# Second feed-forward layer: half of the second parts of groups 9 and 10 as a third, half as wide chunk of seven products, the other half plain at the end

## Chip, cores and metric

One NeuronCore of one Trainium2 chip runs the whole program in one launch. The metric is the device time of one execution, in microseconds (us); the figure for a kernel is the median of several runs. One execution of the kernel before was recorded by the hardware profiler, and all rows below come from it.

## What is computed

A decoder layer of width 1024 over 1024 tokens in 32-bit floating point: a SwiGLU feed-forward half-step, a mixing layer, a second SwiGLU half-step and a final RMSNorm. What the change touches is the second half-step and the norm behind it:

```
def swiglu(h, w_gate, w_up, w_down):
    return (jax.nn.silu(h @ w_gate) * (h @ w_up)) @ w_down
...
        h = modulate(rms_norm(x, ffn2_norm[l]), sh3, sc3)
        x = x + 0.5 * g3[:, None, :] * swiglu(h, ffn2_w_gate[l], ffn2_w_up[l], ffn2_w_down[l])
    return rms_norm(x, final_norm)
```

`w_gate` and `w_up` are 1024x2816, `w_down` is 2816x1024. The kernel cuts the inner width 2816 into 11 groups of 256, numbered 0 to 10. The **first part** of a group is its gate and up products, `silu(h @ w_gate) * (h @ w_up)`; the **second part** is its share of the product with `w_down`.

## The kernel before, in words

**Numbers.** Every 32-bit operand is kept as two `float32r` halves, a rounded one and the rest. A product is three matmuls, high by high, high by low and low by high (`mm3`). Tokens are cut into two halves of 512 (`h` = 0 and 1), and a matmul is 128 by 128 weights against 128x512 activations, into one PSUM bank.

**Seven products.** Groups 1 to 10 of the first part run by Winograd's form of Strassen's scheme. The activations are cut into four blocks A11, A12, A21, A22 (token half by half of the inner dimension). From them come four combinations S1 to S4, sums and differences of blocks, each made from earlier ones, and seven products take the place of eight: A11, S1, S2, S4, S3, A12, A22, in that order (`SEVEN`), in three PSUM accumulators named B, C and A (`fbd_0C` is accumulator C for output column pair 0). The weights need combinations too. They are made in DRAM-to-SBUF transfers: a raw tile is loaded by a DMA that SyncE (SP) issues, and another block is added onto it by an accumulating DMA that GpSimd (POOL) issues (line 173). `Weights.seven` makes seven weight tiles of four blocks: the raw tile x takes one addition, the raw tile y takes three, each after the tile before it was split. `Weights.pump` splits a raw tile into a weight tile `w` with a `CAST` on ScalarE (ACT) and a subtraction on VectorE (DVE), in the fixed order of the granules, whenever one of the weight slots comes free. Three raw tiles are held at a time.

**Second part.** `seven` leaves a group's A blocks, and its S combinations, in DRAM (`Kept`): each block is split into its two halves on ACT and DVE into a tile of the pool `movA` (20 tiles of 512 KB) and written by SP (`kept9A` is a write of an A block of group 9, `kept9S` of an S combination). `down7` then does the second part of four groups at once, a *chunk*: chunk 0 is groups 1 to 4, chunk 1 groups 5 to 8. `fetch_chunk` reads the kept blocks back, one block of one group per DMA of 512 KB (`fb1lA` is a block A of group 1), into tiles that the first part, or the chunk before, has just finished with. A chunk has two passes p = 0 and 1; each does the seven products of four of the eight output columns `d`, 7 products x 2 columns x 4 groups x 3 = 168 matmuls. Each finished result goes through one more addition on DVE and is added into `x` by a `SCALAR_TENSOR_TENSOR`.

**End of the kernel.** Groups 9 and 10 are not in a chunk. Group 9 keeps only its four A blocks in DRAM, and group 10 keeps its own in SBUF as `fb_0a` and `fb_1a`. Behind chunk 1 a plain loop (`for dh in range(2)`) does the second part of both: two halves `dh` of four columns each, 2 token halves, 4 matmul triples per column. Each finished column goes to `after2`, which squares it for the final norm (ACT), sums the squares (POOL) and scales `x` (ACT). The last token half of the second `dh` is cut into two pieces of 256 tokens, so that the norm of one piece runs beside the matmuls of the other.

**Order of work.** In this part of the program the instructions are put in order by a scheduler, from the program's order, the dependences and the free tiles of each pool; the order in which the code calls things is only its starting point. Each engine, and the queue of DMA issues on SP, then runs its own list strictly in that order. SP has eight semaphores for its DMAs, used in turn, and a DMA waits for the one eight places before it.

Of the kernel before, what the change touches and what calls it, by code (L numbers as in the profile page):

```python
# [21 lines left out]
P = 128  # L22
# [14 lines left out]
CHUNKS = 2  # L37

LAST = ((0, NGRP - 2, NGRP - 1), (NGRP - 2, NGRP - 1))
# [80 lines left out]
class Weights:  # L120
# [51 lines left out]
    def add(self, r, src):  # L172
        self.G.dma_start(out=r[:], in_=src, accum_op=ALU.add)  # L173

    def load(self, upto):
        while len(self.raws) < min(upto, len(self.srcs)):
            i = len(self.raws)
            r = self.raw_pool(i).tile([P, 1024], F32, tag="raw", name=f"raw{i}")
            src, more = self.srcs[i]
            self.SP.dma_start(r[:], src)  # L180
            if more is not None:
                self.add(r, more)
            self.raws.append(r)
# [6 lines left out]
    def pump(self):  # L190
        while self.slots and len(self.tiles) < len(self.granules):
            i = len(self.tiles)
            j, more = self.granules[i]
            self.load(j + 1)
            src = self.raws[j][:]
# [33 lines left out]
def hymba_layer(ctx: ExitStack, tc, x_d, xt_d, wm1_d, wmod_d, gu1_d, gs1_d, ds1_d, wl1_d, win_d, wout_d, glu_d, gu2_d, gs2_d, wd2_d, ds2_d, wl2_d, cols_d, cond_d, lam_d, bc_d, out_d):  # L229
# [29 lines left out]
    def ps(name):  # L259
        return mm_ps.tile([P, HALF], F32, tag="mm", name=name)  # L260
# [26 lines left out]
    def stream(gu, gs, wd, ds, wl, m):  # L287


        for g in range(m):  # L290
            plain([gu[2 * g], gu[2 * g + 1]])
        for g in range(m, NGRP):
            ws.seven(gs[g - m], [wd[:, q, :] for q in range(2)] if g == 1 and wd is not None else (), g == 1 and wd is None)
        for c in range(CHUNKS):
            for p in range(2):
                ws.seven(ds[c, p])
        plain([wl[i] for i in range(wl.shape[0])])

    stream(gu1_d, gs1_d, None, ds1_d, wl1_d, SEVEN_FROM[0])
    plain([win_d[i] for i in range(8)] + [glu_d] + [wout_d[i] for i in range(4)])  # L300
    stream(gu2_d, gs2_d, wd2_d, ds2_d, wl2_d, SEVEN_FROM[1])
# [406 lines left out]
    def down7(name, lefts, n_, then=None, first=None):  # L708

        for p in range(2):  # L710
            bank, t1, c1, u2 = {}, {}, {}, {}

            def update(i, h, half, src):
                d = 2 * p + i + 4 * half
                by = (minus if half else gate)[:, n_, d : d + 1]
                V.scalar_tensor_tensor(out=x[d][h], in0=src[:], scalar=by, in1=x[d][h], op0=ALU.mult, op1=ALU.add)

# [7 lines left out]
            for n, (left, b) in enumerate(SEVEN):  # L725
                (w,) = ws.take()
                for i in range(2):
# [3 lines left out]
                    for k in range(4):  # L731
                        mm3(bank[b, i][:], w, 4 * (k // 2) + 2 * (k % 2) + i, lefts[left][k], opens and k == 0, k == 3, more=not opens)
# [605 lines left out]
    lefts = [{left: [] for left, _ in SEVEN} for _ in range(CHUNKS)]  # L1338
# [3 lines left out]
    def fetch_chunk(c, left, name="fa"):  # L1342
        for g in range(1 + 4 * c, 5 + 4 * c):
            lefts[c][left].append(fetch(kept[g], left, HOMES[left], f"{name}{g}l"))
# [333 lines left out]
    kept = {g: kept_for(g, g not in LAST[1], True) for g in range(1, NGRP - 1)}  # L1678
    HOMES = dict(A11="B", S2="A", A12="B", S3="A", S1="B", A22="A", S4="A")
    lefts = [{left: [] for left in HOMES} for _ in range(CHUNKS)]  # L1680
    a_last = {}

    def fetch_last(left):
        if left == "A11":
            for h in range(2):
                for fi in range(2):
                    a_last[fi, h] = fetch(kept[NGRP - 2], f"A{h + 1}{fi + 1}", "B", f"fb{NGRP - 2}l")

    seven("fb1", lambda: down2(a_prev, 2, "fb0", (0, 1)), kept[1])
# [9 lines left out]
    def after2(d, h, tok):  # L1699
        n = tok.stop - tok.start  # L1700
        if d == 0:
# [3 lines left out]
        ss.add(xs, apart=d == KT - 1, beside=d < 7)  # L1705
# [17 lines left out]
        if d == KT - 1:  # L1723
            ss.rstd(D, use, 6, 11)

    for dh in range(2):
        wd = ws.take(2)
        for h in range(2):
            for tok in PIECES[h] if dh else WHOLE:
                for i in range(4):  # L1730
                    d = 4 * dh + i
                    o = ps(f"fb10d{d}_{h}_{tok.start}")
                    for q, (w, a) in enumerate(zip(wd, (a_last, a_prev))):
                        for fi in range(2):
                            mm3(o[:, tok], w, 4 * fi + i, a[fi, h], q == fi == 0, q == fi == 1, tok)
                    xs = x[d][h][:, tok]
                    V.scalar_tensor_tensor(out=xs, in0=o[:, tok], scalar=gate[:, 2, d : d + 1], in1=xs, op0=ALU.mult, op1=ALU.add)
                    for piece in PIECES[h] if not dh else [tok]:
                        after2(d, h, piece)
        ws.free(2)  # L1740
# [18 lines left out]
def _arrays(i):  # L1759
# [7 lines left out]
    for n in (1, 2):  # L1767
# [4 lines left out]
        b = wd.reshape(NGRP, 2, P, 2, 512)  # L1772
        if n == 2:
            a["wd2"] = b[0].transpose(1, 2, 0, 3).reshape(P, 2, 1024)
        b = b[list(LAST[n - 1])].transpose(3, 0, 2, 1, 4).reshape(-1, 2, P, 1024)
        a[f"wl{n}"] = b.transpose(0, 2, 1, 3)

        b = wd.reshape(NGRP, 2, P, 2, 2, 2, P)[1 : 1 + 4 * CHUNKS].reshape(CHUNKS, 2, 2, 2, P, 2, 2, 2, P)
        b = b.transpose(0, 6, 1, 4, 3, 5, 2, 7, 8)

        b = [b[:, :, :, :, q, r].reshape(CHUNKS, 2, 2, P, 512).swapaxes(2, 3).reshape(CHUNKS, 2, P, 1024) for q, r in FOUR]
        a[f"ds{n}"] = np.stack(b, axis=2)
# [23 lines left out]
_ORDER = ["x", "xt", "wm1", "wmod", "gu1", "gs1", "ds1", "wl1", "win", "wout", "glu", "gu2", "gs2", "wd2", "ds2", "wl2", "cols", "cond", "lam", "bc"]  # L1806
# [17 lines left out]
```

## Time and profile before

| | us |
|---|---|
| median of 3 runs (1685.75 to 1691.35) | 1690.64 |
| the profiled execution, its own time | 1691.52 |
| its span, first to last instruction | 1689.7 |
| TensorE (PE) busy in the span | 1657.2 |
| VectorE (DVE) busy | 1065.5 |
| ScalarE (ACT) busy | 676.8 |
| first product of chunk 0 starts | 1478.01 |
| first product of chunk 1 starts | 1554.17 |
| plain loop starts | 1630.33 |
| last six matmuls of the plain loop: start, duration | 1677.31, 0.88 |

All lines of the trace that read `L111` or `L173` come from a helper that issues for all callers, so an instruction is told by its tiles: what it writes, an arrow, what it reads. A row of the timeline has the start in us from the span's start, the duration, the engine, the operation, the tiles, the shapes, how many instructions are merged in it, and in square brackets the idle time of the engine before it with what ended it. `SPq` is the queue of DMA issues on SP; its row tells when a transfer was issued, not when it landed.

### The profile page before, as it was taken

What the parts mean: (1) busy time and instruction counts of PE and PEld (TensorE: products, weight loads), DVE (VectorE), ACT (ScalarE), POOL (GpSimd) and SP (SyncE); (2) the same over time, 40 slices, a digit from 0 to 9 for tenths busy, and PEclk for the clock granted to TensorE, in tenths of its full rate; (3) what the DMA queues carried; (4) which work ended last, traced back from release to release, by engine and by line L of the source; (5) the groups of instructions that cost most, each with busy time, mean ns of one, the idle gap of its engine ahead of it and who ended that gap; (6) DMA issues with size and microseconds to landing.
All of it is one profiled execution on the core that took longest, in us unless ns stands there. A gap on an engine that the chain in (4) does not pass through costs nothing.

```text
span 1689.7 us, 20647 instructions
## 1 busy us (share of the span) xinstructions
PE 1657.2 (98%) x7521; PEld 1364.8 (81%) x7521; DVE 1065.5 (63%) x1581; ACT 676.8 (40%) x992; POOL 169.4 (10%) x207
## 2 busy tenths in 40 slices
PE   8999989999999999999999999999999999999997
PEld 5888878878888888787878778888888888888887
DVE  7984787766567758735656848856555655444454
ACT  6654333333454431332214316434444444322234
POOL 2010000001001102100000121000001101010003
PEclk9999999999999999999999999999999999999999
DMA  9477987987898767145653324558887787989812
GB/s 352 136 165 180 263 253 210 271 235 202 258 315 232 183 210 281 39 112 163 199 158 110 103 97 150 133 140 220 239 227 206 218 222 218 321 271 341 263 55 100
DMA packets 129128, 340.21 MB, mean 201 GB/s; under 512 B 22401, under 2 KB 38017, under 8 KB 128002
## 3 DMA queue, kind: packets, MB, share of 16 engines
q1 hardware_dynamic: 112898, 280.16, 47.9%
q0 software_dynamic: 16128, 58.73, 20.1%
q8 instruction: 59, 0.97, 0.2%
q14 instruction: 43, 0.35, 0.1%
HBM read 254.41 MB, written 76.02 MB: 196 GB/s over the span
## 4 chain that ended last, share of the span: by engine, by line
PE 70%; DVE 7%; DMA 6%; issue 2%; SPq 1%; ACT 0%; POOL 0%; DVEq 0%; POOLq 0%; ACTq 0%
PE fald L111 4%; PE wo L111 3%; PE fad_0B L111 3%; PE fbd_0B L111 3%; PE fad_1B L111 3%; PE fbd_1B L111 3%; PE fb10d L111 2%; PE u L111 2%; PE b L111 2%; DMA wm<-in_wmod 2%; DMA swx<-X 2%; PE c L111 1%; DMA raw<-in_gs 1%; PE fad_0C L111 1%; PE fb0u L111 1%
## 5 line engine op out<-in xcount | busy, mean ns | idle before, releaser
L111 DVE TENSOR_TENSOR w<-raw,w 128x1024 fp32r<-128x1024 f32 x242 | 296.3, 1226 | 264.2 <-ACT w L111 263.9
L111 ACT CAST w<-raw 128x1024 fp32r<-128x1024 f32 x242 | 254.0, 1051 | 310.9 <-DMA raw<-in_ds 60.2
L173 POOL DMA_DIRECT2D raw<-in_gs x80 | 70.6, 885 | 741.9 <-DVE w L111 454.0
L111 DVE CUSTOM_DVE_ANT_0 wm<-wm,cact 128x1024 f32<-128x1024 f32 x56 | 76.0, 1370 | 36.3 <-DMA wm<-in_wmod 31.6
L173 POOL DMA_DIRECT2D raw<-in_ds x32 | 28.1, 877 | 281.4 <-DVE w L111 178.6
L111 PE MATMUL p<-h,w 128*128 128x512 f32 x192 | 49.4, 407 | 1.3 <-ACT h L111 1.0
L111 PE MATMUL wo<-oa,w 128*128 128x512 f32 x192 | 45.5, 391 | 2.9 <-ACT w L111 2.2
L111 PE MATMUL wo<-ob,w 128*128 128x512 f32 x192 | 45.6, 392 | 1.1 <-ACT ob L111 0.6
L111 PE MATMUL v<-h,w 128*128 128x512 f32 x192 | 46.0, 393 | 0.0
L111 PE MATMUL c<-h,w 128*128 128x512 f32 x192 | 46.0, 393 | 0.0
L111 PE MATMUL b<-h,w 128*128 128x512 f32 x192 | 45.1, 392 | 0.0
L111 PE MATMUL u<-h,w 128*128 128x512 f32 x192 | 44.8, 392 | 0.2 <-DVE h L111 0.2
L111 PEld LDWEIGHTS wo<-oa,w 128*128 128x128 f32 x192 | 35.8, 188 | 11.1 <-ACT w L111 2.6
L111 PEld LDWEIGHTS p<-h,w 128*128 128x128 f32 x192 | 35.7, 192 | 9.6 <-ACT h L111 1.6
L111 PEld LDWEIGHTS wo<-ob,w 128*128 128x128 f32 x192 | 35.7, 188 | 9.2 <-ACT ob L111 1.0
L111 PEld LDWEIGHTS u<-h,w 128*128 128x128 f32 x192 | 35.7, 188 | 8.3 <-DVE h L111 0.6
L111 PEld LDWEIGHTS b<-h,w 128*128 128x128 f32 x192 | 35.7, 188 | 7.2
L111 PEld LDWEIGHTS v<-h,w 128*128 128x128 f32 x192 | 35.5, 188 | 7.1
L111 PEld LDWEIGHTS c<-h,w 128*128 128x128 f32 x192 | 35.5, 188 | 7.0
L111 DVE SCALAR_TENSOR_TENSOR x<-fb10d,gate,x 128x512 f32<-128x512 f32 (+1 forms) x20 | 12.9, 643 | 24.4 <-PE fb10d L111 24.3
L111 DVE TENSOR_TENSOR X<-co,X 128x512 f32<-128x512 f32 x8 | 5.5, 692 | 35.3 <-DMA swx<-X 27.5
L111 PE MATMUL fb10d<-fb9lA,w 128*128 128x512 f32 (+1 forms) x120 | 25.6, 347 | 0.0
(1532 smaller groups left out, 3866.5 us busy)
## 6 DMA issues: line engine op xcount, KB each, us to landing
raw<-in_gs SPq DMA_DIRECT2D x80, 512.0 KB, 4.9
raw<-in_gs POOLq DMA_DIRECT2D x80, 512.0 KB, 6.6
wm<-in_wmod SPq DMA_DIRECT2D x56, 512.0 KB, 6.8
raw<-in_ds SPq DMA_DIRECT2D x32, 512.0 KB, 5.9
raw<-in_ds POOLq DMA_DIRECT2D x32, 512.0 KB, 7.3
mw<-in_wm SPq DMA_DIRECT2D x8, 1024.0 KB, 8.9
raw<-in_win SPq DMA_DIRECT2D x16, 512.0 KB, 4.3
raw<-in_wl SPq DMA_DIRECT2D x10, 512.0 KB, 4.3
```

What stands on the lines that cost most here:

```text
L111: r = getattr(self.engine, name)(*args, **kw)
L173: self.G.dma_start(out=r[:], in_=src, accum_op=ALU.add)
```

## The change

Group 9 and group 10 now keep all seven blocks in DRAM, as groups 1 to 8 do, and form a third chunk of two groups. Only its first pass is run by seven products (columns 0, 1, 4, 5): 7 x 2 x 2 x 3 matmuls, with weights half as wide (128x512 raw tiles). Columns 2, 3, 6 and 7 stay plain, in one loop at the end that is built as the second `dh` was. `after2` now starts a sum of squares at whichever column comes first, since the columns no longer come in the order 0 to 7.

```
-CHUNKS = 2
-LAST = ((0, NGRP - 2, NGRP - 1), (NGRP - 2, NGRP - 1))
+CHUNKS = ((1, 2, 3, 4), (5, 6, 7, 8)), ((1, 2, 3, 4), (5, 6, 7, 8), (9, 10))
+LAST = (0, NGRP - 2, NGRP - 1), (NGRP - 2, NGRP - 1)
+ENDS = 2, 3, 6, 7
...
             w = pool.tile([P, 2, 1024], F32R, tag="w", name=f"w{i}")
-            hi, lo = w[:, 0, :], w[:, 1, :]
+            hi, lo = (w[:, q, : src.shape[-1]] for q in range(2))
...
-    def down7(name, lefts, n_, then=None, first=None):
-        for p in range(2):
+    def down7(name, lefts, n_, then=None, first=None, passes=range(2), after=None):
+        for p in passes:
...
-    kept = {g: kept_for(g, g not in LAST[1], True) for g in range(1, NGRP - 1)}
+    kept = {g: kept_for(g, True, True) for g in range(1, NGRP)}
...
-    for g in range(2, NGRP - 1):
-        seven(f"fb{g}", kept=kept[g])
-    a_prev = seven("fb10", then=lambda left: fetch_chunk(0, left, "fb"))
+    for g in range(2, NGRP):
+        seven(f"fb{g}", kept=kept[g], then=(lambda left: fetch_chunk(0, left, "fb")) if g == NGRP - 1 else None)
+    a21 = []
+    def fetch_ends(left):
+        fetch_chunk(2, left, "fb")
+        if left == "A11":
+            a21.extend(fetch(kept[g], "A21", "A", f"fb{g}l") for g in LAST[1])
     down7("fbd0", lefts[0], 2, lambda left: fetch_chunk(1, left, "fb"))
-    down7("fbd1", lefts[1], 2, fetch_last)
+    down7("fbd1", lefts[1], 2, fetch_ends)
...
+    down7("fbd2", lefts[2], 2, passes=(0,), after=after3)
+    wd = ws.take(2)
+    for h in range(2):
+        for tok in PIECES[h]:
+            for i, d in enumerate(ENDS):
...
+                for q, w in enumerate(wd):
+                    for fi in range(2):
+                        act = lefts[2][f"A{h + 1}{fi + 1}"][q] if (h, fi) != (1, 0) else a21[q]
+                        mm3(o[:, tok], w, 4 * fi + i, act, q == fi == 0, q == fi == 1, tok)
```

The matmuls up to chunk 0 keep their order. Two places behind that come out otherwise than before.

**Place 1: the middle of chunk 0's first pass.** The queue of SP before the change, from the fetches of block S4 of groups 1 to 4 to the load of raw weight 141 (`fb1lS4` is block S4 of group 1, read from `kept1S4`):

```order
L111 DMA fb1lS4_11358<-kept1S4_8568 128x1024
L111 DMA fb2lS4_11360<-kept2S4_8576 128x1024
L111 DMA fb3lS4_11362<-kept3S4_8584 128x1024
L111 DMA fb4lS4_11364<-kept4S4_8592 128x1024
L111 DMA fb1lS3_11401<-kept1S3_8566 128x1024
L111 DMA fb2lS3_11403<-kept2S3_8574 128x1024
L111 DMA fb3lS3_11405<-kept3S3_8582 128x1024
L111 DMA fb4lS3_11407<-kept4S3_8590 128x1024
L111 DMA raw141_11445<-in_ds2 128x1024
```

The same stretch of SP's queue after the change:

```order
L113 DMA fb1lS4_11391<-kept1S4_8568 128x1024
L113 DMA kept10A12_8636<-fb10A12_11383 128x1024
L113 DMA fb2lS4_11393<-kept2S4_8576 128x1024
L113 DMA fb3lS4_11395<-kept3S4_8584 128x1024
L113 DMA fb4lS4_11397<-kept4S4_8592 128x1024
L113 DMA kept10A22_8633<-fb10A22_11427 128x1024
L113 DMA fb1lS3_11435<-kept1S3_8566 128x1024
L113 DMA fb2lS3_11437<-kept2S3_8574 128x1024
L113 DMA fb3lS3_11439<-kept3S3_8582 128x1024
L113 DMA fb4lS3_11441<-kept4S3_8590 128x1024
L113 DMA kept10A11_8634<-fb10A11_11473 128x1024
L113 DMA raw141_11480<-in_ds20 128x1024
```

Three writes of group 10's blocks (A12, A22, A11) now stand between the fetches; each can be issued only when its block has been split. Raw weight 141 and, behind it, the fetches of block A12 have moved behind them.

PE in the same pass before the change, where `fbd0_0_0C` and `fbd0_0_1C` are accumulator C of the two columns:

```order
L111 MATMUL fbd0_0_0C_11532<-fb4lS4_11364,w214_11527 128x512 x3
L111 MATMUL fbd0_0_1C_11547<-fb1lS4_11358,w214_11527 128x512 x3
L111 MATMUL fbd0_0_1C_11547<-fb2lS4_11360,w214_11527 128x512 x3
L111 MATMUL fbd0_0_1C_11547<-fb3lS4_11362,w214_11527 128x512 x3
L111 MATMUL fbd0_0_1C_11547<-fb4lS4_11364,w214_11527 128x512 x3
L111 MATMUL fbd0_0_0B_11497<-fb1lS3_11401,w211_11397 128x512 x3
L111 MATMUL fbd0_0_0B_11497<-fb2lS3_11403,w211_11397 128x512 x3
```

PE there after the change:

```order
L113 MATMUL fbd0_0_0C_11588<-fb4lS4_11397,w214_11583 128x512 x3
L113 MATMUL fbd0_0_0A_11721<-fb1lA12_11482,w215_11618 128x512 x2
L113 MATMUL fbd0_0_1A_11736<-fb1lA12_11482,w215_11618 128x512 x2
L113 MATMUL fbd0_0_0A_11721<-fb1lA12_11482,w215_11618 128x512
L113 MATMUL fbd0_0_1A_11736<-fb1lA12_11482,w215_11618 128x512
L113 MATMUL fbd0_0_0A_11721<-fb2lA12_11484,w215_11618 128x512 x3
L113 MATMUL fbd0_0_1A_11736<-fb2lA12_11484,w215_11618 128x512 x3
L113 MATMUL fbd0_0_0A_11721<-fb3lA12_11486,w215_11618 128x512 x3
L113 MATMUL fbd0_0_1A_11736<-fb3lA12_11486,w215_11618 128x512 x3
L113 MATMUL fbd0_0_0A_11721<-fb4lA12_11488,w215_11618 128x512 x3
L113 MATMUL fbd0_0_1A_11736<-fb4lA12_11488,w215_11618 128x512 x3
L113 MATMUL fbd0_0_1C_11603<-fb1lS4_11391,w214_11583 128x512 x3
```

All 24 matmuls of block A12 (two columns by four groups by three) now stand between the two columns of S4; before, they stood behind both columns of S4 and all of S3.

**Place 2: the weights of chunk 0's second pass.** SP's queue before the change, where raw weights 142 to 145 are the four of the second pass:

```order
L111 DMA fb4lA22_11495<-kept4A22_8585 128x1024
L111 DMA raw142_11530<-in_ds2 128x1024
L111 DMA raw143_11565<-in_ds2 128x1024
L111 DMA raw144_11599<-in_ds2 128x1024
L111 DMA raw145_11698<-in_ds2 128x1024
```

After the change, from the last fetch of block A22 on:

```order
L113 DMA fb4lA22_11531<-kept4A22_8585 128x1024
L113 DMA raw142_11586<-in_ds20 128x1024
L113 DMA kept10S1_8637<-fb10S1_11534 128x1024
L113 DMA kept10S3_8638<-fb10S3_11539 128x1024
L113 DMA kept10S2_8639<-fb10S2_11544 128x1024
L113 DMA kept10S4_8640<-fb10S4_11549 128x1024
L113 DMA raw143_11621<-in_ds20 128x1024
L113 DMA raw144_11655<-in_ds20 128x1024
```

Raw weight 143 now stands behind the four writes of group 10's S combinations.

DVE there before the change, where `w218` is the tile that is split from raw weight 143 and `t1` the temporaries of block A12:

```order
L111 TENSOR_TENSOR w218_11661<-raw143_11565,w218_11661 128x1024
L111 TENSOR_TENSOR fbd0_0_0t1_11510<-fbd0_0_0t1_11510,fbd0_0_0A_11665 128x512
L111 SCALAR_TENSOR_TENSOR x0_0_3747<-fbd0_0_0t1_11510,gate_95,x0_0_3747 128x512
L111 TENSOR_TENSOR fbd0_0_1t1_11525<-fbd0_0_1t1_11525,fbd0_0_1A_11680 128x512
L111 SCALAR_TENSOR_TENSOR x0_0_3747<-fbd0_0_1t1_11525,gate_95,x0_0_3747 128x512
L111 TENSOR_TENSOR w219_11695<-raw142_11530,w219_11695 128x1024
```

DVE after the change, from the two updates of `x` by the results of A12 to the split of S4 (the additions into the two `t1`, which read accumulator A, stand right ahead of these rows):

```order
L113 SCALAR_TENSOR_TENSOR x0_0_3747<-fbd0_0_0t1_11566,gate_95,x0_0_3747 128x512
L113 SCALAR_TENSOR_TENSOR x0_0_3747<-fbd0_0_1t1_11581,gate_95,x0_0_3747 128x512
L113 TENSOR_TENSOR fbd0_0_0u2_11636<-fbd0_0_0u2_11636,fbd0_0_0C_11588 128x512
L113 SCALAR_TENSOR_TENSOR x2_0_3749<-fbd0_0_0u2_11636,minus_96,x2_0_3749 128x512
L113 TENSOR_TENSOR fb10S1_11534<-fb10uc1_11298,fb10S1_11534 128x512
L113 TENSOR_TENSOR fb10S3_11539<-fb10c21_11502,fb10S3_11539 128x512
L113 SCALAR_TENSOR_TENSOR fb10uc1_11298<-fb10uc1_11298,fb10ut1_11255 128x512
L113 TENSOR_TENSOR fbd0_0_1u2_11650<-fbd0_0_1u2_11650,fbd0_0_1C_11603 128x512
L113 SCALAR_TENSOR_TENSOR fb10uu2_11340<-fb10uu2_11340,fb10uc1_11298 128x512
L113 TENSOR_TENSOR fb10S2_11544<-fb10uc1_11298,fb10S2_11544 128x512
L113 SCALAR_TENSOR_TENSOR x2_0_3749<-fbd0_0_1u2_11650,minus_96,x2_0_3749 128x512
L113 TENSOR_TENSOR fb10S4_11549<-fb10uu2_11340,fb10S4_11549 128x512
```

The splits of S1, S3, S2 and S4 of group 10 now stand in this list behind A12's results and among those of S4 and S2, and the last of the four is the fourteenth operation counted from the first addition into `t1`.

More of the change, by code (lines that the diff above doesn't have):

```diff
@@ L716, in update @@
                 V.scalar_tensor_tensor(out=x[d][h], in0=src[:], scalar=by, in1=x[d][h], op0=ALU.mult, op1=ALU.add)
+                if after is not None:
+                    after(d, h)
             def copied(dst, b, i, nm):
@@ L730, in down7 @@
                         bank[b, i] = ps(f"{name}_{p}_{i}{b}")
-                    for k in range(4):
-                        mm3(bank[b, i][:], w, 4 * (k // 2) + 2 * (k % 2) + i, lefts[left][k], opens and k == 0, k == 3, more=not opens)
+                    m = len(lefts[left])
+                    for k in range(m):
+                        mm3(bank[b, i][:], w, 2 * k + i, lefts[left][k], opens and k == 0, k == m - 1, more=not opens)
                     if n == 0:
@@ L1337, in hymba_layer @@
     clock.period = 2
-    lefts = [{left: [] for left, _ in SEVEN} for _ in range(CHUNKS)]
+    lefts = [{left: [] for left, _ in SEVEN} for _ in CHUNKS[0]]
     a_last = [{} for _ in LAST[0]]
@@ L1342, in fetch_chunk @@
     def fetch_chunk(c, left, name="fa"):
-        for g in range(1 + 4 * c, 5 + 4 * c):
+        for g in CHUNKS[name == "fb"][c]:
             lefts[c][left].append(fetch(kept[g], left, HOMES[left], f"{name}{g}l"))
@@ L1700, in after2 @@
         n = tok.stop - tok.start
-        if d == 0:
+        if (h, tok.start) not in n4:
             n4[h, tok.start] = Sumsq(f"n4_{h}_{tok.start}", n, acc_in_mov)
@@ L1704, in after2 @@
         xs = x[d][h][:, tok]
-        ss.add(xs, apart=d == KT - 1, beside=d < 7)
+        ss.add(xs, apart=ss.count == KT - 1, beside=ss.count < 7)
         A.activation(xs, xs, AF.Copy, scale=cols[:, C_NF + d : C_NF + d + 1])
@@ L1772, in _arrays @@
         b = wd.reshape(NGRP, 2, P, 2, 512)
+        e = wd.reshape(NGRP, 2, P, 2, 2, 2, P)[list(LAST[1]), :, :, :, 1]
         if n == 2:
```

65 lines of the change are left out of this document (27 added, 38 removed).

## The prediction

> **What bounds the kernel now.** I began with the page: how busy each engine is over the span.
>
> ```profile
> span 1689.7 us, 20647 instructions
> PE 1657.2 (98%) x7521; PEld 1364.8 (81%) x7521; DVE 1065.5 (63%) x1581; ACT 676.8 (40%) x992; POOL 169.4 (10%) x207
> ```
>
> TensorE (PE) is the bound over the whole span. What counts is whether that holds where the change works, so next I cut the end of the kernel into stretches. The columns are the stretch, its length, busy time with instructions of PE, PEld, DVE, ACT and POOL, the granted clock, the DMA share and GB/s.
>
> ```profile
> 1480.00:1500.00 20.00, 20.00 (x90) 16.53 (x90) 6.91 (x8) 7.83 (x11) 0.86 (x1) 1.00 1.03 392
> 1500.00:1520.00 20.00, 20.00 (x90) 16.57 (x89) 13.12 (x16) 4.79 (x5) 2.98 (x4) 1.00 0.64 154
> 1560.00:1580.00 20.00, 20.00 (x89) 16.54 (x89) 6.49 (x7) 6.35 (x9) 0.68 (x1) 1.00 1.02 388
> 1620.00:1640.00 20.00, 20.00 (x90) 16.57 (x89) 11.22 (x14) 6.05 (x8) 1.28 (x1) 1.00 0.01 2
> ```
>
> PE has no idle time, at full clock. But the DMA engines are full too around 1490 and 1570, where a chunk's blocks are fetched, and nearly empty behind 1620. So an added or delayed transfer costs nothing at the end of the kernel and may cost much near chunk 0. Third, PE's timeline: where each product starts.
>
> ```profile
> 1494.33 0.84 PE L111 MATMUL fbd_0C<-fb1lS,w 128*128 128x512 f32 x3
> 1497.05 0.84 PE L111 MATMUL fbd_1C<-fb1lS,w 128*128 128x512 f32 x3
> 1505.21 0.84 PE L111 MATMUL fbd_0A<-fb1lA,w 128*128 128x512 f32 x3
> 1521.53 0.84 PE L111 MATMUL fbd_0C<-fb1lS,w 128*128 128x512 f32 x3
> 1526.97 0.84 PE L111 MATMUL fbd_0B<-fb1lS,w 128*128 128x512 f32 x3
> ...
> 1630.33 1.52 PE L111 MATMUL fb10d<-fb9lA,w 128*128 128x512 f32 x6
> 1631.69 1.52 PE L111 MATMUL fb10d<-fb_0a,w 128*128 128x512 f32 x6
> ```
>
> Six matmuls of 512 take 1631.69 - 1630.33 = 1.36 us, 0.227 each. Half a product (one column, 12 matmuls) takes 2.72, a whole one 5.44. S4's two halves start at 1494.33 and 1497.05, A12 at 1505.21, and the second and third product of the second pass at 1521.53 and 1526.97.
>
> **What the change saves.** Four columns of groups 9 and 10 took 4 x 2 x 4 x 3 = 96 matmuls of 512 and take 84 by seven products. Twelve fewer at 0.227: **-2.7 us**, certain, since PE is gap-free there. The other four columns stay as they were, two token halves and the pieces included, so what follows the last matmul stays too. Chunk 2's 16 fetches and smaller weights fall behind 1590, where the DMA has room.
>
> **What it adds near chunk 0.** Twelve more writes of 512 KB (four of group 9, eight of group 10), and they stand in SP's queue between transfers that PE needs soon. SP's queue before, and how long such transfers take (issues: name, count, size, median us to landing):
>
> ```profile
> 1461.19 0.42 SPq L111 DMA_DIRECT2D fb2lS<-kept2S  x1
> 1475.98 0.33 SPq L111 DMA_DIRECT2D raw<-in_ds  x1
> 1477.48 0.32 SPq L111 DMA_DIRECT2D fb1lA<-kept1A  x1
> 1486.26 0.32 SPq L111 DMA_DIRECT2D fb3lA<-kept3A  x1
> 1487.48 0.32 SPq L111 DMA_DIRECT2D fb4lA<-kept4A  x1
> 1492.57 0.33 SPq L111 DMA_DIRECT2D raw<-in_ds  x1
> ...
> fb1lA<-kept1A SPq DMA_DIRECT2D x3, 512.0 KB, 12.5
> kept9A<-fb9A SPq DMA_DIRECT2D x3, 512.0 KB, 3.5
> raw<-in_gs SPq DMA_DIRECT2D x1, 512.0 KB, 4.2
> ...
> raw<-in_ds POOLq DMA_DIRECT2D x4, 512.0 KB, 8.9
> ...
> raw<-in_ds POOLq DMA_DIRECT2D x3, 512.0 KB, 5.5
> ```
>
> Full, the queue moves one transfer per 1487.48 - 1486.26 = 1.22 us, and each waits until it lands after 12.5; a lone write lands after 3.5, so 2.3 of that is latency. A raw load on an emptier queue takes 4.2. The last two rows are POOL's additions onto raw weights: in the stretch 1458 to 1490, with SP's queue full, 8.9; in 1500 to 1515, with SP quiet, 5.5. So the two sorts cost each other some 3.4 us.
>
> *A, block A12.* Behind the fetch of fb1lS4 the queue now holds the write of group 10's A12, whose split (a cast on ACT, a subtraction on DVE) stands behind the split of weight 212 on both engines. Those two rows before, and the rows for short operations:
>
> ```profile
> 1473.64 1.05 ACT L111 CAST w<-raw 128x1024 fp32r<-128x1024 f32 x1 [1.01 <-DMA raw<-in_ds]
> 1474.73 1.22 DVE L111 TENSOR_TENSOR w<-raw,w 128x1024 fp32r<-128x1024 f32 x1
> 1512.36 0.68 DVE L111 TENSOR_TENSOR fbd_1t<-fbd_1t,fbd_1A 128x512 f32<-128x512 f32 x1
> 1513.07 0.75 DVE L111 SCALAR_TENSOR_TENSOR x<-fbd_1t,gate,x 128x512 f32<-128x512 f32 x1
> 1519.01 0.59 ACT L111 COPY fbd_0t<-fbd_0B 128x512 f32<-128x512 f32 x1 [1.02 <-PE fbd_0B L111]
> ```
>
> So that write leaves at 1474.73 + 1.22 + 0.68 = 1476.6 at the earliest, and up to 5 us later (1481.6) because four writes of group 9's S blocks (4 x 1.22) now precede the raw weights. Before, SP issued the next S4 fetch at 1461.19: it now stands still for 15 us or more. Behind the write come three S4 fetches, a write, four S3 fetches, a write, raw weight 141 and A12's first fetch, twelve in all: 12 x 1.22 + 2.3 = 16.9, so A12 lands at 1493.5 to 1498.5, plus about 3 for a POOL addition beside it, 1496.5 to 1501.5. Weight 141, one place ahead, needs a cast and a subtraction (2.3), ready about 1 us after A12. PE, which took A12 at 1505.21, now wants it at 1497.05, after S4's first half. Stall 0.5 to 5.5; I take **4**, nearer the top, since the writes of group 9 are certain.
>
> *B, S4's second half.* It accumulates onto a bank that ACT must copy out first, into a buffer which A12's result holds until `x` is updated. From A12's last matmul: two additions and an update on DVE (0.68 + 0.68 + 0.75) and the copy (0.59), 2.7, less what overlaps, about 2.3. A22 now follows S3 directly and waits for S3's addition on DVE (0.68). **3** (2.3 to 3.4).
>
> *C, the second pass's weights.* Call E the end of A12's matmuls: 1497.05 + 4 + 5.44 = 1506.5. Raw weight 143 stands on SP behind the write of group 10's S4, whose split is the fourteenth DVE operation after E, 14 x 0.70 = 9.8 (DVE's own list; 0.70 is the spacing 1512.36 to 1513.07). With 0.4 for PE's last matmul and the issue it leaves at E + 10.2, about 1516.7, where it was 1492.57 before: 24 us later. The path from there, in rows of before:
>
> ```profile
> 1503.16 1.80 POOL L173 DMA_DIRECT2D raw<-in_ds  x2 [18.85 <-DMA raw<-in_ds]
> 1508.74 1.05 ACT L111 CAST w<-raw 128x1024 fp32r<-128x1024 f32 x1 [6.34 <-DMA raw<-in_ds]
> 1511.28 1.05 ACT L111 CAST w<-raw 128x1024 fp32r<-128x1024 f32 x1 [1.48 <-DMA raw<-in_ds]
> 1513.74 1.22 DVE L111 TENSOR_TENSOR w<-raw,w 128x1024 fp32r<-128x1024 f32 x1
> 1518.02 1.23 DVE L111 TENSOR_TENSOR w<-raw,w 128x1024 fp32r<-128x1024 f32 x1 [0.98 <-ACT w L111]
> ```
>
> POOL issues the additions onto weights 143 and 142 at 1503.16; the second product's weight (219) is ready at 1513.74 + 1.22 = 1514.96, 11.8 later, against PE's 1521.53: 6.6 of slack, which a delay of 24 us eats. After the change: a landing of 4.2 and the 11.8, ready at E + 10.2 + 16.0 = E + 26.2. PE arrives after S4's second half, S3, A22 and A11 of the second pass: E + 2.72 + 3 x 5.44 + B's 3 = E + 22. Stall 4.2. That holds if the additions run alone, as they did at 1503.16. But chunk 1's fetches are issued right behind weight 144, so the loaded price holds: 3.4 more, and 3.4 again if each of the two additions pays it. Stall 4.2 to 11; I take **8**. The Trainium skill ("DMA: Bandwidth & Descriptors", section "Issuing engines are not separate DMA queues") says that transfers from SP and GpSimd run on the same 16 DMA engines and interleave. By that rule the loaded price holds and the stall is the 8; with engines of POOL's own it would be 4.2. The trace agrees, 8.9 against 5.5.
>
> *D, the third product's weight (220).* It needs another addition onto raw weight 143, after weight 218's split. It was ready at 1518.02 + 1.23 = 1519.25, 4.3 after 219; with the loaded price 7.7, against 5.44 of PE work: 2.3, and 3.4 more if it pays twice. None if unloaded. I take **3** (0 to 5.7).
>
> **Sum.** 4 + 3 + 8 + 3 = 18 of stalls, less 2.7: +15.3. On the profiled execution's 1691.5 (span 1689.7, the rest around it) that is 1706.8. The median of the runs lies 0.9 lower, inside their scatter; I forecast **1706.5**. The lower ends give 0.5 + 2.3 + 4.2 + 0 - 2.7 = +4.3, 1695.8; the upper ones 5.5 + 3.4 + 11 + 5.7 - 2.7 = +22.9, 1714.4. The same page, in section "Bandwidth", limits transfers with HBM to about 358 GB/s per core. By that a 512 KB transfer would take 1.46 us and A would be some 3 us longer (an estimate from that page). The trace moved 392 in a 20 us stretch, so its 1.22 stands.
>
> **The rivals.**
>
> *Covered after all (not slower).* SP gets to weight 143 early enough: it would have to be issued within 6.6 us of 1492.57, about 1499. Then A to D vanish and 1691.5 - 2.7 = 1688.8 is left. For it speaks that PE has no gap today with the DMA full. Against it, the fourteen operations on DVE behind A12: A12 cannot end before 1497.05 + 5.44 = 1502.5. Chance 0.07.
>
> *Only the end suffers.* Chunk 2's weights are used every 2.72 instead of 5.44, while the three additions onto its y tile follow each other. If one link costs as much as an unloaded one plus a short cast and subtraction (5.5 + 0.59 + 0.68 = 6.8) against two uses (5.44), that is 1.3 a link, some 4 in all: with the stalls at chunk 0 small, 1691.5 - 2.7 + 4 to 6, about 1694. Against it, half-width transfers should be shorter, and several weights are ready ahead. Chance 0.10.
>
> *It rolls on.* The second pass is late by 15, and chunk 1's fetches, which wait for the tiles of chunk 0, collide with the additions for its weights as C does: another 5 to 10, 1712 to 1717. Against it, chunk 1's blocks start from tiles freed at PE's own pace, which was enough before. Chance 0.10.
>
> **How the numbers follow.** My forecast has 0.73. The range 1695 to 1715 takes in both ends of the sum and half of the two slower rivals; outside lie "covered" and the rest of them, 0.2 in all. A measurement here tells about 0.3%, 5 us, from no change. Slower by more than that, over 1695.7: the forecast, the third rival and a small part of the second, 0.87. Within: "covered" and the rest of the second, 0.11. Faster by 0.3% would need twice the saving: 0.02.
>
> **What would show it.** Right: `fbd_0A` before `fbd_1C` with PE idle just ahead of it; SP without an issue from about 1465 to 1477 or later; raw weight 143 issued near 1517; the longest idle time of PE ahead of the second pass's `fbd_0C`, ended by the split of a weight; no gap of PE from chunk 1 to the pieces. Wrong: no idle time of PE between 1490 and 1560, or idle time mainly behind 1600.

## The result and the profile after

The changed kernel takes 1707.88 us (median of 4, 1704.34 to 1709.24) against 1689.97 before: a ratio of 1.0107, 95% interval 1.0083 to 1.0131. It is slower by 17.9 us, where 16 (to 1706.5) was forecast. The profiled execution took 1707.87, its span is 1706.1, against 1689.7 before. One profiled execution of an experiment below (plain_end) ran at a granted clock of 0.65 throughout; none of its rows is used.

From the page of the changed kernel: span, and PE's line.

```profile
span 1706.1 us, 20735 instructions
PE 1662.6 (97%) x7509; PEld 1368.0 (80%) x7509; DVE 1081.9 (63%) x1608; ACT 685.7 (40%) x1011; POOL 172.8 (10%) x211
```

There are 12 matmuls fewer (7509 for 7521) and yet 5.4 us more busy time: some matmuls seem to have become slower. The page cannot say which; the stretches can (columns as in the prediction).

```profile
1480.00:1500.00 20.00, 16.90 (x75) 13.67 (x73) 5.55 (x7) 5.01 (x8) 0.86 (x1) 1.00 0.99 331
1500.00:1520.00 20.00, 15.64 (x55) 12.41 (x56) 11.53 (x17) 6.99 (x10) 0.00 (x0) 0.83 0.81 331
1520.00:1540.00 20.00, 14.82 (x60) 11.91 (x59) 7.45 (x9) 3.06 (x4) 2.63 (x3) 0.89 0.92 279
1540.00:1560.00 20.00, 19.14 (x78) 15.02 (x77) 8.32 (x9) 7.20 (x9) 1.72 (x2) 0.94 0.98 313
1620.00:1640.00 20.00, 20.00 (x90) 16.57 (x89) 8.31 (x11) 4.97 (x8) 1.73 (x2) 1.00 1.03 348
```

Two things are to be seen between 1480 and 1560. PE's busy time is below 20 in each stretch: it waits. And the granted clock, 1.00 in every stretch before, is 0.83 to 0.94 in three of them. Behind 1620 PE is full again although the DMA engines now are as well (1.03, where they had 0.01). Next, the timeline of PE in the changed kernel; the bracket is the idle time ahead of a row and what ended it.

```profile
1502.30 1.19 PE L113 MATMUL fbd_0A<-fb1lA,w 128*128 128x512 f32 x2 [5.40 <-DMA fb1lA<-kept1A]
...
1504.14 0.63 PE L113 MATMUL fbd_0A<-fb1lA,w 128*128 128x512 f32 x1
1504.57 0.63 PE L113 MATMUL fbd_1A<-fb1lA,w 128*128 128x512 f32 x1
...
1512.85 0.97 PE L113 MATMUL fbd_1C<-fb1lS,w 128*128 128x512 f32 x3 [2.06 <-ACT fbd_1c L113]
...
1537.37 1.22 PE L113 MATMUL fbd_0C<-fb1lS,w 128*128 128x512 f32 x2 [5.18 <-ACT w L113]
...
1545.77 0.73 PE L113 MATMUL fbd_0B<-fb1lS,w 128*128 128x512 f32 x2 [0.33 <-ACT w L113]
1547.03 0.50 PE L113 MATMUL fbd_0B<-fb1lS,w 128*128 128x512 f32 x1 [0.53 <-DVE w L113]
...
1573.93 0.84 PE L113 MATMUL fbd_0B<-fb5lA,w 128*128 128x512 f32 x3
...
1694.36 0.88 PE L113 MATMUL fb10d<-fb10lA,w 128*128 128x256 f32 x6
```

All idle time lies at the four places A to D: 5.40, 2.06, 5.18 and 0.33 + 0.53, together 13.50. Behind a long gap the matmuls start 1504.57 - 1504.14 = 0.43 apart instead of 0.227: A12's 24 take 8.49 (1502.30 to 1512.85 - 2.06) instead of 5.44. From 1573.93, chunk 1's first matmul, there is no gap up to the pieces' sums. Last, SP's queue in the changed kernel, with the writes of group 10 and what follows each.

```profile
1465.45 0.32 SPq L113 DMA_DIRECT2D fb1lS<-kept1S  x1
1479.08 0.32 SPq L113 DMA_DIRECT2D kept10A<-fb10A  x1
...
1491.44 0.39 SPq L113 DMA_DIRECT2D fb1lA<-kept1A  x1
...
1503.42 0.33 SPq L113 DMA_DIRECT2D raw<-in_ds  x1
1515.60 4.59 SPq L113 DMA_DIRECT2D kept10S<-fb10S  x4
1520.24 1.20 SPq L113 DMA_DIRECT2D raw<-in_ds  x2
```

What SP waited for between 1440 and 1540 (total, times, longest), as far as group 10 is concerned:

```profile
SPq L113 <- DVE fb10A L113: 17.4, 2, 12.4
SPq L113 <- DVE fb10S L113: 14.0, 4, 10.9
```

For 13.6 us, between 1465.45 and 1479.08, SP issues nothing: it stands at the write of A12, whose block is not made yet (12.4 of it is the wait for the split on DVE). It stands a second time, 5.0, at the write of A22. A12's first fetch leaves at 1491.44 and lands when PE starts, 1502.30. Between 1503.42 and 1515.60 it stands again, at the S writes, and raw weights 143 and 144 leave behind them.

### The profile page after: what moved, and what is told of

It is laid out like the page before. It is cut to its first block, busy times and chain, and to the rows that moved or that the text cites. A ratio compares the mean times of both kernels' runs of the same rounds, so it can differ in the third digit from the quotient of the medians.

```text
span 1706.1 us, 20735 instructions
## 1 busy us (share of the span) xinstructions
PE 1662.6 (97%) x7509; PEld 1368.0 (80%) x7509; DVE 1081.9 (63%) x1608; ACT 685.7 (40%) x1011; POOL 172.8 (10%) x211
## 4 chain that ended last, share of the span: by engine, by line
PE 77%; DVE 9%; DMA 9%; issue 2%; ACT 1%; SPq 1%; POOL 0%; DVEq 0%; POOLq 0%; ACTq 0%
PE fald L113 3%; DMA raw<-in_ds 3%; PE fad_1B L113 3%; PE fad_0B L113 3%; PE p L113 3%; DMA wm<-in_wmod 2%; PE wo L113 2%; PE b L113 2%; PE fbd_1B L113 2%; PE fbd_0B L113 2%; PE u L113 2%; DVE w L113 2%; PE fad_1C L113 1%; PE fad_0C L113 1%; DMA swx<-X 1%
## 5 line engine op out<-in xcount | busy, mean ns | idle before, releaser
L113 DVE TENSOR_TENSOR w<-raw,w 128x1024 fp32r<-128x1024 f32 (+1 forms) x247 | 298.5, 1211 | 280.4 <-ACT w L113 271.8
L113 ACT CAST w<-raw 128x1024 fp32r<-128x1024 f32 (+1 forms) x247 | 256.0, 1039 | 319.9 <-DMA raw<-in_ds 87.7
L113 PE MATMUL fb0u<-h,w 128*128 128x512 f32 x96 | 23.8, 391 | 0.0
L113 PE MATMUL fb0g<-h,w 128*128 128x512 f32 x96 | 23.2, 389 | 0.0
```

The source lines that it names most:

```text
L113: r = getattr(self.engine, name)(*args, **kw)
```

## The experiments

The theory: group 10's writes stand in SP's queue ahead of transfers that PE needs sooner, and SP waits there for the blocks. The rivals: the bytes of twelve more writes in a stretch with full DMA engines, or the third chunk itself. Each run is compared with the kernel before on the same chip. For all of them at once, "chunk 0" is the time from PE's first matmul of chunk 0 to its first of chunk 1, "idle" PE's idle time in it, and "slow" the rest of its growth over the 76.16 before: matmuls at a lower clock, and some 0.3 at each gap in which the last matmul runs out and the next ones start (an estimate from the starts of the matmuls).

| kernel | ratio to before, 95% interval | chunk 0 | idle | slow |
|---|---|---|---|---|
| before | 1 | 76.16 | 0 | 0 |
| after | 1.0107 (1.0083 to 1.0131) | 96.23 | 13.50 | 6.57 |
| plain_end | 1.0121 (1.0103 to 1.0139) | | | |
| plain_end_again | one execution | 96.05 | 12.44 | 7.45 |
| late_a | 1.0051 (1.0034 to 1.0068) | 89.46 | 8.60 | 4.70 |
| late_s | 1.0049 (1.0034 to 1.0064) | 89.04 | 8.49 | 4.39 |
| late_both | 1.0024 (1.0011 to 1.0037) | 83.86 | 3.80 | 3.90 |
| nine_s | 0.9994 (0.9981 to 1.0007) | 76.16 | 0 | 0 |
| own_queue | 1.0034 (1.0023 to 1.0046) | 86.03 | 7.27 | 2.60 |
| a22_later | 1.0003 (0.9992 to 1.0015) | 78.75 | 1.26 | 1.33 |
| one_buffer | 1.0095 (1.0069 to 1.0121) | 92.70 | 11.50 | 5.04 |
| fill_gap | one execution | 97.98 | 10.34 | 6.72, and 4.76 of added matmuls |

**plain_end and plain_end_again: the writes without the third chunk.** The kernel before, with groups 9 and 10 written in full and their A blocks fetched for the plain end:

```diff
-    kept = {g: kept_for(g, g not in LAST[1], True) for g in range(1, NGRP - 1)}
+    kept = {g: kept_for(g, True, True) for g in range(1, NGRP)}
...
+        if left == "S2":
+            for h in range(2):
+                for fi in range(2):
+                    a_prev[fi, h] = fetch(kept[NGRP - 1], f"A{h + 1}{fi + 1}", "A", f"fb{NGRP - 1}l")
...
-    a_prev = seven("fb10", then=lambda left: fetch_chunk(0, left, "fb"))
+    seven("fb10", kept=kept[NGRP - 1], then=lambda left: fetch_chunk(0, left, "fb"))
```

> All seven blocks of groups 9 and 10 are written, as in the changed kernel, but the end is the plain one of the kernel before (groups 9 and 10 at full width, their A blocks fetched). Theory (the writes of group 10 stand in SP's queue ahead of transfers that PE needs soon): the same stalls as in the changed kernel, 5.4 ahead of A12 and 5.2 ahead of the second pass's S1, and 2.7 us more matmul work: 1707.9 + 2.7 = 1710.6, between 1708 and 1713. Rival (the third chunk with its half-wide weights is what costs): without it about the time before, under 1695.

> The same kernel as plain_end, for a profile at full clock. Theory: with no third chunk at all, PE waits where it waits in the changed kernel: 5.4 for A12's block, 2.1 ahead of S4's second half, about 5 ahead of the second pass's S1, about 1 ahead of S2, each within 1; about 1710.6. Rival (the third chunk costs): none of these waits.

Measured: 1708.86, 1710.31 and 1713.62 us, and 1708.13 in the one execution of plain_end_again. That execution's timeline of PE:

```profile
1499.70 1.19 PE L111 MATMUL fbd_0A<-fb1lA,w 128*128 128x512 f32 x2 [5.26 <-DMA fb1lA<-kept1A]
1509.26 0.96 PE L111 MATMUL fbd_1C<-fb1lS,w 128*128 128x512 f32 x3 [2.06 <-ACT fbd_1c L111]
1534.92 1.22 PE L111 MATMUL fbd_0C<-fb1lS,w 128*128 128x512 f32 x2 [4.71 <-ACT w L111]
1544.41 0.50 PE L111 MATMUL fbd_0B<-fb1lS,w 128*128 128x512 f32 x1 [0.41 <-DVE w L111]
```

The four waits are there without any third chunk. That rival is out; the chunk itself only saves.

**late_a, late_s, late_both: the place of the writes.** Writes of group 10 are put into a list `late`, and `flush(n)` issues the first `n` of it. The edit of late_both; late_a has `flush()` for `flush(4)` and no change of `down7`; late_s has `if name != "fb10" or left[0] == "A":` and `flush(0)`:

```diff
-                    SP.dma_start(self.dram[left][:], t[:].bitcast(F32))
+                    late.append((self.dram[left], t))
+                    if name != "fb10":
+                        flush()
...
+    flush(4)
...
-    down7("fbd0", lefts[0], 2, lambda left: fetch_chunk(1, left, "fb"))
+    down7("fbd0", lefts[0], 2, lambda left: fetch_chunk(1, left, "fb"), lambda left: flush(100 if left == "S2" else 0))
```

> The changed kernel with one thing moved: the four writes of group 10's A blocks are issued behind the fetches of chunk 0, the four S writes as they were. Theory: SP has no hole of 13 us at 1465 to 1479, A12 lands before PE wants it, the stall of 5.4 ahead of it goes and the 2.9 of slow matmuls behind that stall too; A12 then ends 8.3 earlier, the S writes and raw weight 143 follow it as before, so the stall ahead of the second pass's S1 stays at about 5: 1707.9 - 8.3 = 1699.6, between 1696 and 1703. Rival (it is the bytes of twelve more writes in a stretch where the DMA engines are full, not their place in the queue): no change, 1704 to 1708.

> The changed kernel with one thing moved: the four writes of group 10's S blocks are issued behind raw weights 143 and 144, the A writes as they were. Theory: the stall of 5.4 ahead of A12 stays, with its slow matmuls and the 2.1 ahead of S4's second half; raw weight 143 is issued near 1505 instead of 1520, so the stalls of 5.2 and 0.9 and the 2.5 of slow matmuls behind them go: 1707.9 - 8.6 = 1699.3, between 1696 and 1703. Rival (bytes): no change, 1704 to 1708.

> The changed kernel with both moved: A writes behind chunk 0's fetches, S writes behind raw weights 143 and 144. Theory: both long stalls go, what is left is at most the 2.1 ahead of S4's second half and what the fuller DMA engines cost: 1690 to 1694, against 1689.97 before. Rival (bytes): 1704 to 1708. Rival (each move only hands its stall on to the next one): 1699 or more, no better than with one moved.

Measured: 1698.61, 1698.51 and 1693.46 us. The bytes are the same in all three, so bytes alone are not the cause, and each move takes away its own stall. In late_a, SP's queue and PE's gaps:

```profile
1481.63 0.32 SPq L113 DMA_DIRECT2D fb1lA<-kept1A  x1
...
1494.70 4.07 SPq L113 DMA_DIRECT2D kept10A<-fb10A  x4
```
```profile
1494.77 0.70 PE L113 MATMUL fbd_0A<-fb1lA,w 128*128 128x512 f32 x2 [1.33 <-DMA fb1lA<-kept1A]
...
1530.13 0.73 PE L113 MATMUL fbd_0C<-fb1lS,w 128*128 128x512 f32 x2 [2.75 <-ACT w L113]
```

Counted from chunk 0's first matmul (1474.24 in late_a, 1477.70 in the changed kernel), A12's fetch leaves at 7.39 instead of 13.74. Its stall is 1.33 instead of 5.40, with 0.79 more in three pieces inside A12's product; the later one is still there, 2.75. The edit moved one thing more than its expectation says: raw weight 142, which stood ahead of the S writes, now leaves behind them as well, and a wait of 1.07 for the split of a weight is new ahead of the second pass. In late_s it is the other way round:

```profile
1502.40 2.90 SPq L113 DMA_DIRECT2D raw<-in_ds  x3
```
```profile
1501.28 1.19 PE L113 MATMUL fbd_0A<-fb1lA,w 128*128 128x512 f32 x2 [6.17 <-DMA fb1lA<-kept1A]
...
1532.63 0.50 PE L113 MATMUL fbd_0C<-fb1lS,w 128*128 128x512 f32 x1 [0.26 <-DVE w L113]
```

Together they bring 14.4 of the 17.9, less than 9.3 + 9.4. Part of that is argued, not tried: the stall at A12 and the one at weight 219 are partly the same lateness, since the S writes follow A12's end. Part of it is a new wait of 2.66 in late_a and late_both; in late_both:

```profile
1504.37 0.61 PE L113 MATMUL fbd_1A<-fb4lA,w 128*128 128x512 f32 x2
1507.64 1.65 PE L113 MATMUL fbd_0B<-fb1lS,w 128*128 128x512 f32 x3 [2.66 <-ACT fbd_0u L113]
```
```profile
1504.63 0.62 ACT L113 CAST fb10S<-fb10uc 128x512 fp32r<-128x512 f32 x1 [3.19 <-DMA kept10A<-fb10A]
...
1507.01 0.58 ACT L113 COPY fbd_0u<-fbd_0B 128x512 f32<-128x512 f32 x1 [0.42 <-DVE x L113]
```

The copy that PE waits for starts when DVE has updated `x`. That update needs the last two matmuls of A12's second column, and these now stand behind S4's second half, at 1504.37. A late A write also holds up S1's cast, by 3.19, but that cast is over before the copy can start.

**nine_s: four writes alone.** The kernel before, with group 9's S blocks written as well (`kept_for(g, True, True)`).

> The kernel before with one thing added: the four S blocks of group 9 are written too (nobody reads them); group 10 stays unwritten and the end plain. Theory: four more writes of 1.22 us each, 4.9 us of transfers in a stretch where the DMA engines are nearly full, but none of them waits long for its block, so they are swallowed by the room behind 1500: 1690, between 1689 and 1692. Rival (bytes in the full stretch cost what they take): 1690.2 + 4.9 = 1695.

Measured: 1688.28 us, no gap in chunk 0. One of its stretches:

```profile
1500.00:1520.00 20.00, 20.00 (x90) 16.57 (x89) 11.34 (x15) 3.15 (x3) 2.65 (x3) 1.00 0.79 209
```

Added bytes turn up where there was room, 209 GB/s in 1500 to 1520 instead of 154, and PE's time is full.

**own_queue: the writes from ACT.**

```diff
-                    SP.dma_start(self.dram[left][:], t[:].bitcast(F32))
+                    (A if name == "fb10" else SP).dma_start(self.dram[left][:], t[:].bitcast(F32))
```

> The changed kernel with the eight writes of group 10 issued by ACT instead of SP, at the places where ACT has made the blocks; the rest of the program as it was. Theory (place in SP's queue): SP has no hole any more, raw weight 143 leaves 10 or more earlier, and both long stalls go: 1692, between 1690 and 1696. Rival (a limited number of transfers is out at a time, whoever issues them, so that a late write holds up SP's next ones as well): A12's stall of 5 stays with its slow matmuls, only the later stalls go: 1698 to 1701.

Measured: 1695.84 us. The time lies in the theory's range, but the mechanism is the rival's for A: the stall of 5.5 stays, those at weights 219 and 220 go, and 1.72 are new ahead of A22. A write on ACT's queue, SP's queue, SP's waits (total, times, longest) and PE:

```profile
1489.27 0.33 ACTq L113 DMA_DIRECT2D kept10A<-fb10A  x1
```
```profile
1488.62 0.33 SPq L113 DMA_DIRECT2D raw<-in_ds  x1
1498.18 0.32 SPq L113 DMA_DIRECT2D fb1lA<-kept1A  x1
```
```profile
SPq L113 <- DMA kept10A<-fb10A: 12.9, 4, 9.2
```
```profile
1503.74 1.62 PE L113 MATMUL fbd_0A<-fb1lA,w 128*128 128x512 f32 x3 [5.55 <-DMA fb1lA<-kept1A]
```

SP waits 9.2 for the landing of a write that it did not issue, and A12's fetch leaves only then, at 1498.18. So a late write holds up SP's next transfers even from another queue. The packed trace shows why: each DMA of SP and of ACT ends in one of the same eight semaphores, used in turn. The write that ACT issued at 1489.27 has number 108 and landed at 1497.30; A12's first fetch, on 108 again, left at 1498.18. The limit here is this program's eight semaphores, shared by two queues; whether the chip has one of its own, no run shows.

**a22_later: more of the order.**

```diff
-lambda left: fetch_chunk(0, left, "fb")
+lambda left: (left != "A22" and fetch_chunk(0, left, "fb"), flush(3 if left == "A12" else 0))
...
+    flush(1)
...
+          lambda left: (left == "S1" and fetch_chunk(0, "A22", "fb"), flush(100 if left == "S2" else 0))
```

> The kernel with both sorts of writes moved, and the fetches of A22 moved too, from ahead of chunk 0 to behind its S1 product, so that raw weight 142 stands ahead of them and of three of the A writes. Theory (what is left of the loss is the order of SP's queue): the 2.7 ahead of S3's product and the 0.5 ahead of the second pass's S1 go, and A22, used 27 us behind S1's end at the earliest, still comes in time or 1 to 2 late: 1689 to 1692, level with the kernel before. Rival (the DMA engines are full with twelve more writes, so whatever is put later is missed somewhere): 1693 to 1697.

Measured: 1692.15 us where the kernel before took 1690.6 on that chip, level with it. (The expectation has one thing the wrong way round: the A writes stand ahead of raw weight 142, the A22 fetches behind it.) All that is left of the gaps in chunk 0:

```profile
1524.11 0.73 PE L113 MATMUL fbd_0C<-fb1lS,w 128*128 128x512 f32 x2 [0.73 <-ACT w L113]
1525.37 0.50 PE L113 MATMUL fbd_0C<-fb1lS,w 128*128 128x512 f32 x1 [0.53 <-DVE w L113]
```

1.26 of waits and 1.33 around them eat the 2.7 that were saved; the granted clock is 1.00 throughout this chunk 0, so the 1.33 are not matmuls at half speed. So the change can be had without loss by order alone; no version here beats the kernel before by more than can be measured.

**one_buffer: the wait ahead of S4's second half.**

```diff
+        if "tmp2" in pools and name.startswith("fbd") and name.endswith(('_0_1c1',)):
+            return pools["tmp2"].tile([P, HALF], F32, tag="t2", name=name)
         return tmp.tile([P, HALF], F32, tag="t", name=name)
...
+    pools["tmp2"] = ctx.enter_context(tc.tile_pool(name="tmp2", bufs=1))
```

> The changed kernel with one more buffer of 2 KB a partition for the copy of S4's second bank in the first pass, which otherwise waits until A12's result gives its buffer back. Theory: the 2.1 ahead of S4's second half go, and its 12 matmuls stand ahead of A12, whose wait falls from 5.4 to about 2.7; but A12's fetch, raw weight 143 and the weights after it come no earlier than A12's block lands, so most of it returns as wait for weights 219 and 220: 1704 to 1708, against 1707.9. Rival (the waits add up): 1707.9 - 2.1 - 2.7 - 2 of slow matmuls = 1701.

Measured: 1704.19 us, 3.7 less than the changed kernel and at the low edge of the theory's range. The two were measured beside different runs of the kernel before, and the intervals of their ratios to it overlap (1.0069 to 1.0121, 1.0083 to 1.0131), so the times alone do not show a gain; the timeline shows what changed places.

```profile
1500.62 0.70 PE L113 MATMUL fbd_0A<-fb1lA,w 128*128 128x512 f32 x2 [3.08 <-DMA fb1lA<-kept1A]
...
1514.73 0.73 PE L113 MATMUL fbd_0B<-fb1lA,w 128*128 128x512 f32 x2 [1.54 <-ACT w L113]
...
1532.02 1.22 PE L113 MATMUL fbd_0C<-fb1lS,w 128*128 128x512 f32 x2 [5.97 <-ACT w L113]
```

The 2.06 are gone and A12's wait falls to 3.08, but the wait for weight 219 grows to 5.97, and a new one of 1.54 for weight 217 stands ahead of the second pass. Of the 4.38 of waits that went (2.06, and 5.40 less 3.08), 2.38 came back at other places, since the idle time fell from 13.50 to 11.50 only.

**fill_gap: matmuls where PE would be idle.**

```diff
+                    if name == "fbd0" and (p, n, i) in ((1, 0, 1),):
+                        o = sm([P, HALF], f"warm{p}")
+                        for _ in range(21 if p else 0):
+                            T.matmul(o[:], lhsT=wsel(w, i)[0], rhs=lefts[left][0][0], start=True, stop=True)
```

> The changed kernel with 21 matmuls of 512 put ahead of the second pass's S1 product, where PE stands idle for 5.2; they repeat a block by a weight into a bank of their own that nobody reads. Theory: PE then does not come to that product from idleness, so its 24 matmuls take 5.4 instead of 7.9, at a granted clock of 1.0 instead of 0.89; but the weight of the third product (220) is ready no earlier, so the 2.5 come back as a wait there, and the time stays at 1706 to 1709. Rival (the slow matmuls come from the full DMA engines or from the weight arriving late, not from the idleness): they stay slow, and the time stays too. Rival (stalls and slow matmuls simply add up): 1705.4.

Measured: 1710.7 us in one execution, above what any of the three expected. Of the 2.8 above the changed kernel's profiled execution, 1.08 lie ahead of chunk 0, where the edit does nothing; executions of one kernel scatter by more than these 2.8. The timeline of PE:

```profile
1534.30 4.92 PE L113 MATMUL warm<-fb1lA,w 128*128 128x512 f32 x21
1539.06 0.61 PE L113 MATMUL fbd_0C<-fb1lS,w 128*128 128x512 f32 x2
...
1546.99 0.73 PE L113 MATMUL fbd_0B<-fb1lS,w 128*128 128x512 f32 x2 [1.51 <-ACT w L113]
1548.25 0.50 PE L113 MATMUL fbd_0B<-fb1lS,w 128*128 128x512 f32 x1 [0.53 <-DVE w L113]
...
1549.65 1.48 PE L113 MATMUL fbd_0B<-fb3lS,w 128*128 128x512 f32 x3
```

Coming from other matmuls, S1's product takes 5.89 without its wait (1539.06 to 1546.99 - 1.51, less 0.53) instead of 8.07 (1537.37 to 1545.77 - 0.33), while the DMA engines are as full as before: from 1539 to 1548 they moved 223 GB/s at a granted clock of 1.00, in the changed kernel from 1537 to 1546 209 GB/s at 0.70. Idleness, not the transfers, makes matmuls slow. As the theory has it, the gain returns as 1.51 + 0.53 of wait for weight 220; and that wait makes the next product slow, 1.48 for three matmuls instead of 0.84.

## Why the prediction came out right, step by step

- **Saving (-2.7): right.** From chunk 1's first matmul to the last one of the plain end, in rows of before:

```profile
1554.17 0.84 PE L111 MATMUL fbd_0B<-fb5lA,w 128*128 128x512 f32 x3
...
1677.31 0.88 PE L111 MATMUL fb10d<-fb_1a,w 128*128 128x256 f32 x6
```

  123.14 before, 1694.36 - 1573.93 = 120.43 after: -2.71.
- **A (4, from 0.5 to 5.5): the mechanism right, the size at its upper end.** The write left at 1479.08, inside 1476.6 to 1481.6. PE had A12 at 1502.30, just behind the forecast's latest landing, 1501.5, and the stall was 5.40. late_a shows that it is the write's place: moved, the stall is 1.33. The stall came out inside its range partly by luck: from the write to A12 it took 23.2, where the sum had 16.9, or 19.9 with an addition beside it, and the write left 2.5 ahead of its latest time. The sum had no term for SP's second stand, 5.0 at the write of A22; how much of the difference is that was not separated.
- **B (3): 2.06.** The wait for ACT's copy is there; the further 0.7 ahead of A22 is not. one_buffer shows that it is a buffer, and that giving one more brings back about half of the waits elsewhere.
- **C (8, from 4.2 to 11): the place and the chain right, the size too large, 5.18.** A12 ended at 1510.79, not 1506.5, and raw weight 143 left 9.5 behind that (10.2 forecast). From POOL's addition the changed kernel has:

```profile
1521.99 0.86 POOL L175 DMA_DIRECT2D raw<-in_ds  x1 [34.97 <-DVE w L113]
1525.17 0.89 POOL L175 DMA_DIRECT2D raw<-in_ds  x1 [2.32 <-issue]
```
```profile
1535.32 1.99 ACT L113 CAST w<-raw 128x1024 fp32r<-128x1024 f32 x2 [5.23 <-DMA raw<-in_ds]
```

  10.15 from the second addition to the cast, against 1508.74 - 1503.16 = 5.58 before: the loaded price was paid, but once, as the two additions ran side by side. The Trainium skill ("DMA: Bandwidth & Descriptors", section "Issuing engines are not separate DMA queues") says that transfers issued by SP and by GpSimd run on the same 16 DMA engines and interleave; the trace agrees, 10.15 for 5.58. And PE started when the casts were done (1537.31), because the first two of its three products use the high part alone: the subtraction, which the forecast had in the path, was not waited for. In all, the weight took 9.45 + 4.93 (raw weight 143 from its issue to the second addition) + 10.15 + 1.99 = 26.5 from A12's end, hardly more than the 26.2 that the forecast had without any load, and PE arrived after 21.4 instead of 22. late_s, with that load ahead of the writes, has 0.26 there.
- **D (3): 0.86.** Weight 220 was late, but S1's product was so slow (8.07 for 5.44) that it hid most of that; at full speed, in fill_gap, the wait is 2.04.
- **The missing term: slow matmuls, 6.57 (some 5.6 of it at half clock, an estimate from the starts of the matmuls).** The forecast let PE go on at 0.227 a matmul behind each stall. This was the step that failed: A12's product took 3.05 more than 5.44, S1's 2.63 more, with a granted clock of 0.83 to 0.94 over the stretches of 20. In shorter stretches the clock of the changed kernel is 0.50 from 1501.41 to 1508.24 and from 1535.55 to 1542.37, and 1.00 in all the rest of chunk 0. The Trainium skill ("TensorE: Matmul & The Clock Gate", Part 1) says that an idle window of about 3.4 us halves the clock, and that about as long a busy one restores it. The trace agrees on the halving (0.43 for 0.227) and on the 5 us stalls as its cause; each time the half clock lasted 6.83 us, two windows of 3.41, since PE was busy for only 2.52 and 1.59 us of the first window.
- **Sum.** 18 of waits were forecast; there were 13.50 of waits and 6.57 of slow matmuls, 20.07 in chunk 0. Less 2.71, less 0.31 ahead of chunk 0 (1478.01 to 1477.70) and 0.65 behind the last matmul (1689.7 - 1677.31 = 12.39, now 1706.1 - 1694.36 = 11.74), that is 16.40, and the span grew by 16.4. So the total came out so close by luck, because two errors cancelled: waits too large by 4.5, and 6.57 not thought of.
- **The rivals.** "Covered after all" fails on A; "only the end suffers" and "it rolls on" fail on PE's full rows from 1573.93. Of the signs named, one did not hold: the longest gap is A's, 5.40, not C's 5.18. Raw weight 143 left at 1520.24, 3 behind the 1517 named.

## What to carry to other kernels

A write that waits for its data holds up every transfer behind it on its queue, and one that lands late can hold up another queue that shares its semaphores, as here: before adding one, list what stands behind it and when PE wants that, and put it behind those transfers, since its own result is needed last. Price the stalls along the chain that sets the last weight's readiness, not one by one: part of what is won at an early stall is waited for at a later one. And where PE was never idle, add to each stall of some microseconds the matmuls behind it at half speed; here that was 3 us for a stall of 5.

## What the runs showed that was not expected

- A stall of about 5 us costs about half as much again in slow matmuls (5.40 and 3.05, 5.18 and 2.63). Short stalls do so only at times: 2.06 in the changed kernel was followed by 12 matmuls in 2.86 instead of 2.72, while 2.04 in fill_gap was followed by products at 1.48 for 0.84. The Trainium skill (same page and part) says that the clock's window runs freely, and the traces agree. In chunk 0 of an execution the clock changes only at steps of 3.41 us: the second half-clock stretch of the changed kernel starts 34.14, ten steps, behind the first. In chunk 0 of eleven profiled executions (all but plain_end's), a step at full clock in which PE was busy for up to 0.40 of it (1.38 us) was always followed by one at half clock, and a step with 0.43 of it or more never; a step at half clock was followed by full clock only when PE was busy all through it (0.80 was not enough). So the 2.06 of the changed kernel, which fell across two steps (2.55 and 2.21 us busy), did not halve the clock, and the waits of fill_gap, which left 1.38 in one step, did.
- Twelve more writes of 512 KB cost next to nothing by their bytes, in a stretch where the DMA engines moved 392 GB/s: four of them nothing (0.9994), all twelve with eight placed late (a22_later) no more than the 2.7 saved elsewhere (1.0003). Whether the 2.6 that remain in a22_later's chunk 0 come from the bytes or from the order is open.
- SP waited 9.2 us for the landing of a write that ACT had issued, because both queues use the same eight semaphores.
